# Block sums of x made early and kept in DRAM, and two column pairs moved into the block products

## The chip, the cores and the metric

One Trainium2 chip, of which the kernel uses one core. That core has a matrix engine (PE, with its weight loads shown apart as PEld), a vector engine (DVE), a scalar engine (ACT), GpSimd (POOL) and a queue engine (SP); SP, ACT and POOL issue DMA transfers. Each engine runs its instructions in the order of the program and waits on semaphores for what others make. The metric is the time of one execution on the device in microseconds, taken as the median of several runs. "The profile" is a page made from one execution that was recorded by the hardware; "the trace" is the record behind it.

## The reference, cut to what matters

All numbers are float32; the sequence has 1024 positions, the model 1024 channels.

```python
h = rms_norm(x, g_mix)
z = h @ w_in + b_in                       # 1024 -> 1024+1024+1536+1536+1024+1024
va, ga, xb, gb, sa, sb = split(z)

u = va * sigmoid(ga)
u = causal_depthwise_conv(u, conv_a_w, conv_a_b)       # 31 taps
u = silu(layer_norm(u, ln_g, ln_b))                    # mean over 1024 channels
y_a = u @ w_a_out

v = causal_depthwise_conv(xb, conv_b_w, conv_b_b)      # 4 taps
v = rg_lru(v, ...)                                     # gates per head, a linear scan in position
y_b = (v * gelu(gb)) @ w_b_out

m = sigmoid(sa) * y_a + sigmoid(sb) * y_b
x = x + m @ w_o
x = x + square(relu(rms_norm(x, g_mlp) @ w_1)) @ w_2   # hidden width 4096
out = rms_norm(x, g_final)
```

In the recurrence `rg_lru`, a = exp(log_a) and the input is multiplied by sqrt(-expm1(2 log_a)); the kernel makes these with exponential, tanh and square root on ACT, and the scan itself on DVE.

## The kernel before, in words

Tiles have 128 partitions; channels lie on partitions and positions along the free dimension. A product in full precision is made of three passes: each operand is split into a high part in the format fp32r and a low part (the rest), and high by high, high by low and low by high are added up. The high part is a copy on ACT. The low part is either a subtraction on DVE, or (`split_dma`, L64) a negated copy on ACT to which POOL's accumulating DMA adds the source.

Matrix `w_in` is used in column chunks of 128 columns, named by what they yield: VA and GA (8 chunks each), XB and GB (12 each), SA and SB (8 each).

*First part* (up to 360 us of the span). The list `CH` has 28 chunks: all of XB, VA and GA. A slot `s` of the loop multiplies one chunk (`chunk_mm`, 48 matmuls of 128x512), loads the weights of the chunk two slots on (`w_load`, SP), and splits those of the next (`w_parts`). In the same slots the gates of the 16 heads are multiplied (`head_mm`, at the slots `HS0`), the four-tap convolution is made (`xb_out`, `xb_parts`), and the scans follow group by group, three tiles to a group: `scan_exp` (exponential and tanh), `scan_root` (square root), `scan_in` and `scan_tile` (DVE; the result goes to DRAM tensor `hd`). `EXP` and `lag` say in which slots. A VA chunk and its GA chunk give, by `u_out`, the tile `ut[j]`, the input of the 31-tap convolution.

The convolution `conv(j)` is two steps on ACT and then 48 small ones on DVE, most of 128x512; its result `y` is stored in DRAM tensor `yd`, and POOL adds `yd[j]` into one tile `ysum` (`sum_up`, L603 to L609). The steps are fillers: the kernel writes the order of all engines by hand (`manual_schedule`) with a planner that keeps an estimated time for each engine (`clk`), a list of DVE steps with a time at which they are ready (`later`), and `vector_work`, which issues what is ready up to a given time and fills the rest with convolution steps, unless `taps["hold"]` is set. The planner's times set the order only.

*Second part* (360 to about 630 us). The chunks of GB, SA and SB are multiplied in pairs (`ZPAIRS`, 14 pairs of neighbours) by a block scheme with seven products in place of eight. The order is `zseq`, and each entry is one product of 12 matmuls (`z_mm`). The right operands are blocks of x, or sums of blocks, in high and low parts (`xbh`, `xbl`): products 1, 2 and 3 use the blocks themselves (`xh`, `xl`), products 7, 6, 5 and 4 use sums. The left operands are blocks of the weights or sums of them (`z_load`, `z_sums`, `z_lhs`; tiles `zw`, `zs`, `zo`). `z_post` copies one bank of PSUM into the next (bank "a" to "b" after product 1, "b" to "e" after product 6, where products 5 and 3 are added), and `z_out` applies gelu (GB; multiplied into the scan's result and stored in `hgd`) or sigmoid (SA, SB; stored in `gates`). A bank that is opened by a copy gets a filler matmul first in the first two pairs (`z_bank`).

The sums of blocks of x are made as follows. Normalised x (`xc`, eight tiles) is stored in DRAM tensor `xu` in slot 3. In slots 23 and 25 `x_load` brings back four tiles each, `x_sum` makes four subtractions on DVE a slot later, and `x_parts` splits the sums in slots 25 to 27 and at steps 0, 2 and 4 of `zseq`. Group 3 of the scans has its exponentials in slot 23, its roots a slot later, and its last tile at step 7 of `zseq`.

*Third part.* The output product of the recurrent branch, `b_mm(j)`, j = 0 to 7, of 72 matmuls each. In the middle of j = 2 two pairs of matmuls over `ysum` give the mean of the convolution (`n_parts`, `n_mean`, L1149); then the convolution's tiles `q`, loaded from `yd`, are centred (`n_center`), and at the start of j = 4 `n_var` makes the variance (L1149 again). Then come the product with `w_a_out`, `w_o` and the MLP, which the change does not touch.

Of the kernel before, what the change touches and what calls it, by code (L numbers as in the profile page):

```python
# [15 lines left out]
P = 128  # L16
# [15 lines left out]
def trunk_kernel(ctx: ExitStack, tc: tile.TileContext, x, xt_in, xt_eo, vecs, w_in, w_a_out, w_b_out,  # L32
# [87 lines left out]
    ep = stage.enter_context(tc.tile_pool(name="extra", bufs=1))  # L120
# [285 lines left out]
    xu = dp.tile([2, 4, P, S], F32, name="xu")  # L406
# [75 lines left out]
    def xb_parts(t):  # L482
        if t % 3 == 2:
            vp_[t] = tuple(qp.tile([P, S], F32R, tag="p", name=f"vt{x}{t}", bufs=4) for x in "hl")
        else:
            vp_[t] = T(f"vth{t}", F32R), T(f"vtl{t}", F32R)
# [64 lines left out]
    def scan_exp(g):  # L551
        at("A", 1.28)
        for t in range(3 * g, 3 * g + 3):
# [113 lines left out]
    xq = {}  # L667

    def x_load(c2):

        xq[c2] = {n: ep.tile([P, S], F32, tag="e", name=f"xs{n}_{c2}") if (n, c2) == (21, 0) else T(f"xs{n}_{c2}")
                  for n in (11, 12, 22, 21)}
        for n, a in xq[c2].items():
            nc.sync.dma_start(a, xu[n % 10 - 1, 2 * (n // 10 - 1) + c2])

    def x_sum(c2, ready):
        q = xq[c2]
        for n, a, b in ((11, 12, 11), (12, 22, 12), (22, 22, 11), (21, 21, 22)):
            later(ready, 1.2, nc.vector.tensor_tensor, q[n], q[a], q[b], ALU.subtract)

    def x_parts(c2, *ps):
        for p in ps:
            src = xq[c2][{6: 22, 7: 12, 5: 11, 4: 21}[p]]
            xbh[p][c2] = h = T(f"xs{p}h_{c2}", F32R)
            xbl[p][c2] = l = T(f"xs{p}l_{c2}", F32R)
            if c2 == 0 and p < 6:
                split_dma(src, h, l)
                at("A", 2.0)
            else:
                nc.scalar.activation(h, src, AF.Copy)  # L690
                later(at("A", 1.0), 1.2, nc.vector.tensor_tensor, l, src, h.bitcast(F32),
                      ALU.subtract)

    CH = [XB, VA, GA, XB + 1, XB + 2]
    for js, g in (((1,), 1), ((2,), 2), ((3,), 3), ((4, 5, 6, 7), 4)):
        CH += [c for j in js for c in (VA + j, GA + j)]
        CH += [XB + t for t in range(3 * g, min(3 * g + 3, 12))]
# [41 lines left out]
    ZPAIRS = [GB + 2 * i for i in range(6)] + [SA + 2 * i for i in range(4)]  # L739
    ZPAIRS += [SB + 2 * i for i in range(4)]  # L740
# [4 lines left out]
    def z_load(i, kk):  # L745

        zraw[i, kk] = raw = qp.tile([P, 2, 4, P], F32, tag="p", name=f"zw{i}_{kk}", bufs=4)
        c = ZPAIRS[i]
# [1357 lines left out]
```

## Time and profile before

| | |
|---|---|
| median of 3 runs | 1548.86 us (1547.82 to 1549.61) |
| the profiled execution | 1549.04 us, of which the recorded span is 1547.2 us |
| PE busy | 1535.6 us, 6804 instructions |
| DVE busy | 1214.5 us |
| ACT busy | 903.6 us |
| POOL busy | 188.6 us |
| start of the block products | 360.57 us |
| end of the first output block of the recurrent branch | 645.1 us |
| the mean's first matmul | 668.7 us |

The page gives the busy time of each engine over the whole span; the stages differ, so a table of busy times by stage is read beside it. A row of the view in order of time has start, duration, engine, line, operation, output and input, and in brackets how long the engine was idle before it and what ended that. Several instructions of one kind in a row are put together, with their count. A line of the waits names the waiting engine and instruction, what it waited for, the sum, the count and the longest.

### The profile page before, as it was taken

The numbers are of one execution on the slowest core, as the hardware profiler recorded it, in microseconds if no ns is written. First come the engines' busy times: TensorE is split into PE (matmuls) and PEld (weight loads), VectorE is DVE, ScalarE is ACT, GpSimd is POOL, SyncE is SP. The second block draws the span as 40 slices with busy tenths as digits, with TensorE's granted clock in tenths as the row PEclk, the third lists the DMA queues.
The fourth block names the chain that finished last, engine by engine and source line by source line (L and its number), as shares of the span: only waits on it lengthen the run. The fifth ranks groups of instructions, "written<-read, shape, count | busy, mean of one in ns | idle before, by whom it ended". The sixth has DMA issues, their size and how long they took to land. (4 is left out here: it accounts for less than half of the span.)

```text
span 1547.2 us, 19086 instructions
## 1 busy us (share of the span) xinstructions
PE 1535.6 (99%) x6804; PEld 1264.6 (82%) x6804; DVE 1214.5 (78%) x1641; ACT 903.6 (58%) x1266; POOL 188.6 (12%) x226
## 2 busy tenths in 40 slices
PE   9999999999999999999999999999999999999998
PEld 7878888788888888888888887888888888888886
DVE  6999989999899983468568868765555558888897
ACT  6748677576667667435375777545444475555553
POOL 0000000002222222000022322000000001111110
PEclk9999999999999999999999999999999999999999
DMA  8653554678999889854579978523333779888852
GB/s 348 169 127 95 160 140 134 158 227 214 264 267 256 195 206 259 270 196 126 185 195 306 194 171 198 211 75 124 113 115 111 242 216 229 226 223 223 205 124 109
DMA packets 124943, 294.18 MB, mean 190 GB/s; under 512 B 12464, under 2 KB 30512, under 8 KB 124848
## 3 DMA queue, kind: packets, MB, share of 16 engines
q1 hardware_dynamic: 93312, 213.00, 40.7%
q0 software_dynamic: 31392, 79.71, 28.1%
q8 instruction: 53, 0.87, 0.2%
q14 instruction: 42, 0.34, 0.1%
q10 hardware_dynamic: 144, 0.26, 0.1%
HBM read 152.93 MB, written 58.72 MB: 137 GB/s over the span
## 5 line engine op out<-in xcount | busy, mean ns | idle before, releaser
L735 PE MATMUL z<-xh,win_h 128*128 128x512 f32 x400 | 125.0, 390 | 0.0
L735 PE MATMUL z<-xl,win_h 128*128 128x512 f32 x400 | 123.5, 390 | 0.0
L1873 DVE TENSOR_TENSOR acc<-acc,d 128x1024 f32<-128x1024 f32 x72 | 87.8, 1220 | 33.4 <-PE d L1861 32.7
L735 PE MATMUL z<-xh,win_l 128*128 128x512 f32 x400 | 99.4, 391 | 0.0
L735 PEld LDWEIGHTS z<-xh,win_l 128*128 128x128 f32 x400 | 75.2, 188 | 16.8
L735 PEld LDWEIGHTS z<-xh,win_h 128*128 128x128 f32 x400 | 75.1, 188 | 16.5 <-ACT win_h L68 0.4
L648 DVE SCALAR_TENSOR_TENSOR y<-u,vec,y 128x511 f32<-128x511 f32 (+14 forms) x120 | 88.5, 737 | 0.0
L735 PEld LDWEIGHTS z<-xl,win_h 128*128 128x128 f32 x400 | 75.1, 188 | 15.8
L648 DVE SCALAR_TENSOR_TENSOR yt<-u,vec,yt 128x511 f32<-128x511 f32 (+6 forms) x112 | 82.6, 737 | 0.0
L648 DVE SCALAR_TENSOR_TENSOR y<-yt,csum,y 128x511 f32<-128x511 f32 (+6 forms) x112 | 82.6, 737 | 0.0
L542 ACT ACTIVATE g<-rg,vec 96x1024 f32<-96x1024 f32 x32 | 35.6, 1113 | 79.6 <-PE rg L532 79.6
L1540 ACT ACTIVATE o<-s 128x512 fp32r<-128x512 f32 x58 | 34.7, 623 | 52.8 <-DVE s L1525 31.3
L67 POOL DMA_DIRECT2D win_l<-win_raw x25 | 21.6, 865 | 319.1 <-ACT win_l L66 248.4
L476 DVE SCALAR_TENSOR_TENSOR v<-xb,vec,v 128x1023 f32<-128x1023 f32 (+2 forms) x36 | 46.2, 1282 | 11.4 <-ACT v L467 10.4
L67 POOL DMA_DIRECT2D zo<-zw x42 | 36.2, 862 | 133.6 <-ACT zo L66 125.3
L1121 PE MATMUL yb<-hgl,wb_h 128*128 128x512 f32 x168 | 51.8, 390 | 0.0
L1121 PE MATMUL yb<-hgh,wb_h 128*128 128x512 f32 x168 | 51.8, 389 | 0.0
L66 ACT ACTIVATE zo<-zw 128x512 fp32r<-128x512 f32 x42 | 26.3, 626 | 30.7 <-DMA zw<-in_w_in_dram 8.7
L67 POOL DMA_DIRECT2D db_1l<-wr x7 | 6.0, 860 | 309.8 <-DMA wr<-in_w_dram 254.0
L1121 PE MATMUL yb<-hgh,wb_l 128*128 128x512 f32 x168 | 41.0, 390 | 0.0
L1085 DVE TENSOR_TENSOR o<-s,o 128x512 fp32r<-128x512 f32 x58 | 38.8, 682 | 0.0
L1121 PEld LDWEIGHTS yb<-hgh,wb_h 128*128 128x128 f32 x168 | 31.6, 188 | 6.5
(1795 smaller groups left out, 4672.9 us busy)
## 6 DMA issues: line engine op xcount, KB each, us to landing
w_raw<-in_w_dram SPq DMA_DIRECT2D x36, 512.0 KB, 5.5
fr<-fd SPq DMA_DIRECT2D x32, 512.0 KB, 5.9
wr<-in_w_dram SPq DMA_DIRECT2D x32, 512.0 KB, 6.5
zw<-in_w_in_dram SPq DMA_DIRECT2D x28, 512.0 KB, 5.9
win_raw<-in_w_in_dram SPq DMA_DIRECT2D x25, 512.0 KB, 4.1
win_l<-win_raw POOLq DMA_DIRECT2D x25, 512.0 KB, 4.5
zo<-zw POOLq DMA_DIRECT2D x42, 256.0 KB, 5.6
gates<-zg SPq DMA_DIRECT2D x32, 256.0 KB, 4.0
```

The costliest lines, as they stand in the source:

```text
L66: nc.scalar.activation(l, src, AF.Copy, scale=-1.0)
L67: nc.gpsimd.dma_start(l, src, accum_op=ALU.add)
L476: nc.vector.scalar_tensor_tensor(v[:, d:S], a[:, 0:S - d], cbw_c[:, w * 12 + t:w * 12 + t + 1], v[:, d:S], ALU.mult, ALU.add)
L542: nc.scalar.activation(a, gps.pop((n, gi))[:HD, :], AF.Sigmoid, bias=(ba_c, bx_c)[gi][:, n:n + 1])
L648: nc.vector.scalar_tensor_tensor(o[:, k:], a[:, 0:HS - k], c, o[:, k:], ALU.mult, add)
L735: nc.tensor.matmul(zps[s][:, HALVES[hf]], w[:, k, :], xw[k][part][hf], start=n == 0, stop=n == 23)
L1085: tt(l, src, h.bitcast(F32), ALU.subtract)
L1121: nc.tensor.matmul(ps[hf], a, b[:, HALVES[hf]], start=n == 0, stop=n == len(todo) - 1)
L1540: nc.scalar.activation(o[:, 0], src, AF.Copy)
L1873: tt(acc[p, q2], acc[p, q2], ps, ALU.add)
```

## The change

The sums of blocks of x are made in slots 4 and 6, in place, on the tiles `xc` themselves (`x_sum`), and `xu`, `x_load` and `x_parts` go. `x_make`, in slots 5 to 7, writes the sums to a new DRAM tensor `xsd`: those for products 7 and 6 as a high part (copied by ACT, stored by a DMA that ACT issues) and a low part (subtracted by DVE, stored by SP); those for products 5 and 4 as they are. The stores on SP are collected and issued once a slot (`x_store`). `x_get` loads the parts for product 6 in the last slot and those for product 7 ahead of the block products. `x_raw` loads the sums for products 5 and 4 at steps 0 and 5 of `zseq`, and `x_split` splits them at steps 3 and 4, and 7 and 8 (ACT for the high part, DVE for the low one).

`CH` has 24 chunks: VA and GA number 6 and 7 leave it. They become pairs 6 and 7 of 16 in `ZPAIRS`, each with its VA chunk as the first and its GA chunk as the second of the pair; `z_load` reads them with a stride. `z_branch` forms the convolution's input from the results, and `z_joined` hands it to the planner when both halves are there.

The exponentials of scan tiles 9 and 10 stand in the last slot but one, that of tile 11 at step 2 of `zseq`, the three roots at step 4, and the scans of the tiles at steps 5, 11 and 15. Convolution steps are held back in the first twelve steps of `zseq` rather than two. One filler matmul is left. Four tiles of `xb_parts` come from another pool. The first left operands are made before the last matmuls of the last slot.

```diff
     wp = stage.enter_context(tc.tile_pool(name="weights", bufs=2))
-    ep = stage.enter_context(tc.tile_pool(name="extra", bufs=1))
...
-    xu = dp.tile([2, 4, P, S], F32, name="xu")
+    xsd = dp.tile([4, 2, 2, P, S], F32, name="xsd")
...
     def xb_parts(t):
-        if t % 3 == 2:
+        if t in (2, 5, 8, 9):
...
-    def scan_exp(g):
-        at("A", 1.28)
-        for t in range(3 * g, 3 * g + 3):
+    def scan_exp(g, part=range(3)):
+        if 0 in part:
+            at("A", 1.28)
+        for t in (3 * g + n for n in part):
...
-    xq = {}
-
-    def x_load(c2):
-
-        xq[c2] = {n: ep.tile([P, S], F32, tag="e", name=f"xs{n}_{c2}") if (n, c2) == (21, 0) else T(f"xs{n}_{c2}")
-                  for n in (11, 12, 22, 21)}
-        for n, a in xq[c2].items():
-            nc.sync.dma_start(a, xu[n % 10 - 1, 2 * (n // 10 - 1) + c2])
-
-    def x_sum(c2, ready):
-        q = xq[c2]
-        for n, a, b in ((11, 12, 11), (12, 22, 12), (22, 22, 11), (21, 21, 22)):
-            later(ready, 1.2, nc.vector.tensor_tensor, q[n], q[a], q[b], ALU.subtract)
-
-    def x_parts(c2, *ps):
-        for p in ps:
-            src = xq[c2][{6: 22, 7: 12, 5: 11, 4: 21}[p]]
-            xbh[p][c2] = h = T(f"xs{p}h_{c2}", F32R)
-            xbl[p][c2] = l = T(f"xs{p}l_{c2}", F32R)
-            if c2 == 0 and p < 6:
-                split_dma(src, h, l)
-                at("A", 2.0)
-            else:
-                nc.scalar.activation(h, src, AF.Copy)
-                later(at("A", 1.0), 1.2, nc.vector.tensor_tensor, l, src, h.bitcast(F32),
-                      ALU.subtract)
-
-    CH = [XB, VA, GA, XB + 1, XB + 2]
-    for js, g in (((1,), 1), ((2,), 2), ((3,), 3), ((4, 5, 6, 7), 4)):
-        CH += [c for j in js for c in (VA + j, GA + j)]
-        CH += [XB + t for t in range(3 * g, min(3 * g + 3, 12))]
+    def x_sum(c2):
+        q11, q12, q22, q21 = (xc[i + c2] for i in (0, 4, 6, 2))
+        for o, a, b in ((q11, q12, q11), (q12, q22, q12), (q22, q22, q11), (q21, q21, q22)):
+            later(clk["P"] - 7, 1.2, nc.vector.tensor_tensor, o, a, b, ALU.subtract)
+
+    def x_make(c2, p):
+        src = xc[{5: 0, 7: 4, 6: 6, 4: 2}[p] + c2]
+        if p in RAW:
+            stored.append((xsd[p - 4, c2, 0], src))
+            return
+        h, l = (T(f"xs{p}{n}_{c2}", F32R) for n in "hl")
+        nc.scalar.activation(h, src, AF.Copy)
+        nc.scalar.dma_start(xsd[p - 4, c2, 0], h.bitcast(F32))
+        later(at("A", 1.1), 1.2, nc.vector.tensor_tensor, l, src, h.bitcast(F32), ALU.subtract)
+        stored.append((xsd[p - 4, c2, 1], l.bitcast(F32)))
+
+    stored = []
+
+    def x_store():
+        for a in stored:
+            nc.sync.dma_start(*a)
+        stored.clear()
+
+    def x_get(c2, p):
+        for n, a in enumerate((xbh, xbl)):
+            a[p][c2] = T(f"xb{p}{'hl'[n]}_{c2}", F32R)
+            nc.sync.dma_start(a[p][c2].bitcast(F32), xsd[p - 4, c2, n])
+
+    def x_raw(c2, p):
+        xbl[p][c2] = T(f"xb{p}l_{c2}", F32R)
+        nc.sync.dma_start(xbl[p][c2].bitcast(F32), xsd[p - 4, c2, 0])
+
+    def x_split(c2, p):
+        xbh[p][c2], l = T(f"xb{p}h_{c2}", F32R), xbl[p][c2]
+        nc.scalar.activation(xbh[p][c2], l.bitcast(F32), AF.Copy)
+        later(at("A", 1.06), 1.2, nc.vector.tensor_tensor, l, l.bitcast(F32), xbh[p][c2].bitcast(F32),
+              ALU.subtract)
+
+    NJ = 6
+    CH = [XB + 0, VA + 0, GA + 0, XB + 1, XB + 2, VA + 1, GA + 1, XB + 3, XB + 4, XB + 5, VA + 2, GA + 2, XB + 6, XB + 7, XB + 8, VA + 3, GA + 3, XB + 9, XB + 10, XB + 11, VA + 4, GA + 4, VA + 5, GA + 5]
...
-    ZPAIRS = [GB + 2 * i for i in range(6)] + [SA + 2 * i for i in range(4)]
-    ZPAIRS += [SB + 2 * i for i in range(4)]
+    ZPAIRS = [(c, c + 1) for c in range(GB, SB + 8, 2)]
+    ZPAIRS[6:6] = [(VA + j, GA + j) for j in range(NJ, 8)]
...
         zraw[i, kk] = raw = qp.tile([P, 2, 4, P], F32, tag="p", name=f"zw{i}_{kk}", bufs=4)
-        c = ZPAIRS[i]
-        nc.sync.dma_start(raw, w_in[c:c + 2, :, 4 * kk:4 * kk + 4, :].rearrange("m p k c -> p m k c"))
+        c, d = ZPAIRS[i]
+        nc.sync.dma_start(raw, w_in[c:d + 1:d - c, :, 4 * kk:4 * kk + 4, :].rearrange("m p k c -> p m k c"))
...
                mybir.EngineType.SP, mybir.EngineType.Pool}
-    HS0 = [4 + 5 * (n // 4) + n % 4 for n in range(NH)]
+    HS0 = [(4, 9, 14, 19)[n // 4] + n % 4 for n in range(NH)]
     head_at = {s: n for n, s in enumerate(HS0)}
-    EXP = {head_slot: g for g, head_slot in enumerate(HS0[4 * g + 3] + 1 for g in range(4))}
-    XL = {23: 0, 25: 1}
-    XS = {25: ((x_parts, 0, 6),), 26: ((x_parts, 0, 7, 5),), 27: ((x_parts, 0, 4),)}
+    EXP = {head_slot: g for g, head_slot in enumerate(HS0[4 * g + 3] + 1 for g in range(3))}
+    RAW = (4, 5)
+    XS = {4: ((x_sum, 0),), 5: ((x_make, 0, 5), (x_make, 0, 7)), 6: ((x_make, 0, 6), (x_make, 0, 4), (x_sum, 1)),
+          7: tuple((x_make, 1, p) for p in (5, 7, 6, 4)),
+          NC1 - 2: ((scan_exp, 3, (0, 1)),),
+          NC1 - 1: ((scan_in, 0, 9, 10), (x_get, 0, 6), (x_get, 1, 6))}
     w_load(3)
     head_w(0)
     w_load(4)
-    for c2 in range(4):
-        nc.sync.dma_start(xu[1, c2], xc[4 + c2])
     w_parts(3)
     with tc.manual_schedule(engines=ENGINES):
         for s in range(3, NC1):
             w_load(s + 2)
-            if s in XL:
-                x_load(XL[s])
...
                 head_mm(before, 1)
+            if s == NC1 - 1:
+                z_get(0, z_lhs)
+                z_get(1, z_lhs)
             if s > 3:
                 chunk_mm(s, 18, 24)
+            x_store()
...
                     g = EXP[s - d]
-                    lag = int(g < 3)
+                    lag = 1
...
                     t = 3 * g + d - 2 - lag
-                    if 3 * g <= t < 3 * g + 3 and t < 11:
+                    if 3 * g <= t < 3 * g + 3 and t < 10:
                         later(rooted[t], 4.8, scan_tile, t)
-            if s == NC1 - 1:
-                z_get(0, z_lhs)
-                z_get(1, z_lhs)
-            if s - 1 in XL:
-                x_sum(XL[s - 1], max((r for r, *_ in todo), default=0))
+            if s == NC1 - 2:
+                for i in range(4):
+                    z_load(i // 2, i % 2)
             for f, *a in XS.get(s, ()):
                 f(*a)
-            if s == NC1 - 3:
-                for i in range(4):
-                    z_load(i // 2, i % 2)
-            if s == 3:
-                for c2 in range(4):
-                    nc.sync.dma_start(xu[0, c2], xc[c2])
...
         zb[i, b] = t = zp.tile([P, HS], F32, tag="z", name=f"z{i}{b}")
-        if i < 2 and b in "be":
+        if i == 0 and b == "b":
...
     def z_out(i, m_, hf, src, name):
-        ci = ZPAIRS[i] + m_
+        ci = ZPAIRS[i][m_]
         bias = bin_c[:, ci:ci + 1]
-        if ci < SA:
+        if ci < XB:
+            z_branch(ci, hf, src, bias)
+        elif ci < SA:
...
+    zu, zg = {}, {}
+
+    def z_branch(ci, hf, src, bias):
+        j = ci % GA
+        if j not in zu:
+            zu[j] = T(f"u{j}")
+        d, g = halved(zu[j], hf), src.rearrange("p (n o) -> p o n", o=2)
+        if ci >= GA:
+            zg[j, hf] = g
+            nc.scalar.activation(src, src, AF.Sigmoid, bias=bias)
+            ready = at("A", 0.62)
+            if hf == 0:
+                later(ready, 0.63, nc.vector.tensor_tensor, d, d, g, ALU.mult)
+                z_joined(j)
+        elif hf == 0:
+            nc.scalar.activation(d, g, AF.Identity, bias=bias)
+            at("A", 0.62)
+        else:
+            later(0, 0.68, nc.vector.scalar_tensor_tensor, d, g, bias, zg.pop((j, hf)), ALU.add, ALU.mult)
+            z_joined(j)
+
+    def z_joined(j):
+        if j in ut:
+            fresh.append(j)
+        ut[j] = zu[j]
+
     hb = {}
     def z_h(i, m_, hf):
-        t = ZPAIRS[i] + m_ - GB
-        if t < 12:
+        t = ZPAIRS[i][m_] - GB
+        if 0 <= t < 12:
...
-    ZX = {0: ((x_parts, 1, 7),), 7: ((later, 0, 4.8, scan_tile, 11),), 2: ((x_parts, 1, 5),), 4: ((x_parts, 1, 4),)}
+    ZX = {0: ((x_raw, 0, 5), (x_raw, 1, 5)), 2: ((scan_exp, 3, (2,)),), 3: ((x_split, 0, 5),), 4: ((x_split, 1, 5), (scan_root, 3),),
+          5: ((later, 0, 4.8, scan_tile, 9), (x_raw, 0, 4), (x_raw, 1, 4)), 7: ((x_split, 0, 4),), 8: ((x_split, 1, 4),), 11: ((later, 0, 4.8, scan_tile, 10),),
+          15: ((later, 0, 4.8, scan_tile, 11),)}
...
         z_get(3, z_lhs)
-        u_out(7, zps[NC1 - 2], zps[NC1 - 1])
-        x_parts(1, 6)
+        u_out(NJ - 1, zps[NC1 - 2], zps[NC1 - 1])
+        scan_in(0, 11)
         vector_work(clk["V"])
+        for c2 in range(2):
+            x_get(c2, 7)
...
                     f(*a)
-            taps["hold"] = n < 2
+            taps["hold"] = n < 12
```

## The prediction

> **What bounds the kernel now.** I read the page first, then the waits of PE, a table of the span by stage, and then, at two places, the order in time.
>
> ```profile
> span 1547.2 us, 19086 instructions
> PE 1535.6 (99%) x6804; PEld 1264.6 (82%) x6804; DVE 1214.5 (78%) x1641; ACT 903.6 (58%) x1266; POOL 188.6 (12%) x226
> ```
> ```profile
> PE spare L345 <- POOL ones L114: 1.6, 1, 1.6
> PE gu4a L1297 <- ACT u_late L1351: 1.6, 1, 1.6
> ```
> ```profile
> 43.00:97.00 54.00, 54.00 (x238) 43.72 (x237) 51.88 (x90) 32.32 (x39) 3.67 (x5) 1.00 0.58 151
> 360.00:580.00 220.00, 219.84 (x971) 181.79 (x970) 202.53 (x310) 143.31 (x245) 55.11 (x64) 1.00 0.92 230
> 580.00:645.00 65.00, 65.00 (x287) 53.50 (x286) 28.67 (x32) 41.84 (x63) 10.36 (x12) 1.00 0.94 266
> ```
>
> PE is busy 99% of the span, and the two rows shown are its longest waits, 1.6 us each; neither lies where the change does. So two things can move the time: matmuls that go or come, and a new wait of PE. In the table by stage the columns after the window are PE, PEld, DVE, ACT, POOL, clock, DMA share and GB/s: the clock granted is full, 238 matmuls in 54.00 us make 0.2269 us for one, 971 in 220 make 0.2266. I take 0.2267. The same table gives the slack elsewhere: DVE is full up to 580 us (202.5 of 220) and idle for 36 of the 65 us after it. That gap is what the change uses up.
>
> **What goes and comes on PE.** Four column chunks of the first part go (VA and GA, 6 and 7), at 48 matmuls each: 192. Two pairs of block products come, each 7 products of 12 matmuls, twice over for two row halves, so 84 a pair: 168. Three of the four filler matmuls at the start of a bank go. Net 27 matmuls less at 0.2267 us: **-6.1 us**, all on the path, since PE never rests. The weight loads lie beside PE both times (PEld 82%).
>
> **The block sums.** The eight subtractions on whole x tiles, eight high parts on ACT and the low parts are as many as before, and only stand earlier. Eight stores and eight loads of 512 KB become twelve stores and twelve loads; four of the stores are issued by ACT.
>
> ```profile
> L656 SPq DMA_DIRECT2D yd<-y x8: 319/341/434, 108.0 to 576.2; - x8
> ```
> ```profile
> xu<-xc SPq DMA_DIRECT2D x8, 512.0 KB, 6.5
> xs<-xu SPq DMA_DIRECT2D x8, 512.0 KB, 8.1
> ```
> An issue on SP took 0.32 to 0.43 us, so ACT pays about 1.4 us over three slots, while it is busy 32.3 of 54 us in the stretch 43 to 97: nothing. The two low parts that were built by an accumulating DMA (POOL) now cost two more DVE steps, of the kind of ysuml below (1.22 us). In slots 4 to 8 DVE is nearly full (51.88 of 54), but most of it is filler, steps of the convolution placed where there is room: what comes in pushes those later. The twelve stores stand on SP ahead of weight loads that are issued two slots (a chunk's 48 matmuls alone are 10.9 us a slot) ahead of use; a store of this size landed in 6.5 us, so they are covered, at zero, unless SP stands a whole slot waiting for a low part (a rival below). The loads of the stored parts are issued a slot or more ahead of their use and landed in 8.1 us in the old form: zero.
>
> **Where block products begin.** Counted from the first block product, Z = 360.57 in the old trace:
>
> ```profile
> 360.57 0.39 PE L933 MATMUL z0a<-xh,zo 128*128 128x512 f32 x1
> 380.29 0.39 PE L933 MATMUL z0e<-xs5h,zo 128*128 128x512 f32 x1
> 386.41 0.39 PE L933 MATMUL z0e<-xh,zo 128*128 128x512 f32 x1
> ```
> ```profile
> 366.66 0.58 ACT L971 ACTIVATE z1b<-z1a 128x512 f32<-128x512 f32 x1
> 367.45 0.64 ACT L776 ACTIVATE zo<-zs 128x512 fp32r<-128x512 f32 x1 [0.21 <-DVE zs L453]
> 367.99 1.04 ACT L690 ACTIVATE xs5h<-xs 128x1024 fp32r<-128x1024 f32 x1
> 369.05 1.28 ACT L945 ACT_TABLE_LOAD   x1
> 370.34 0.69 ACT L945 ACTIVATE ze<-z0a,vec 128x512 f32<-128x512 f32 x1
> ...
> 375.05 0.58 ACT L974 ACTIVATE z0e<-z0b 128x512 f32<-128x512 f32 x1
> ```
> ```profile
> 329.03 2.96 ACT L564 ACTIVATE g<-g 128x1024 f32<-128x1024 f32 x3
> ```
> ```profile
> L557 ACT ACTIVATE g<-g,sm 128x1024 f32<-128x1024 f32 x12 | 13.9, 1155 | 0.4
> L556 ACT ACTIVATE a<-g,c 128x1024 f32<-128x1024 f32 x12 | 13.7, 1142 | 0.0
> ```
> The product into bank z0e, due at Z+19.7, needs ACT's copy z0b to z0e, which stood at Z+14.5. In the new order ACT does, from z1b (Z+6.1) on: z1b 0.5, a weight part 0.5, a table load 1.28, exponential and tanh of scan tile 11 (1.15 each), a table load 1.28, a gelu 0.6, a weight part 0.55, the high part of x for block 5 (1.0), a gelu 0.6, two weight parts 1.06, the other high part 1.0, a table load 1.28, three square roots 2.96. That is 14.9 us, so the copy starts at Z+21.0 and ends at Z+21.6: PE waits **1.9 us**. Behind the copy stand, on ACT, zu0 and the parts of the weight sum for the third product of the bank; in the old trace POOL issued that sum's accumulating transfer 1.9 us after the copy's start:
>
> ```profile
> 376.94 0.86 POOL L67 DMA_DIRECT2D zo<-zs  x1 [2.18 <-ACT zo L66]
> ```
> ```profile
> zo<-zw POOLq DMA_DIRECT2D x42, 256.0 KB, 5.6
> zo<-zs POOLq DMA_DIRECT2D x28, 256.0 KB, 6.9
> ```
> So it is issued at Z+22.9 and lands 5.6 to 6.9 us later, at 28.5 to 29.8, where PE wants it at Z+25.8 (386.41). The two waits are one chain, and the later end counts: 2.7 to 4.0 us; if the transfer keeps ahead, the 1.9 alone; if ACT overlaps better than I sum, less. I take **+3.3** (range 1 to 4).
>
> [...]
>
> **The convolution's end and the mean.** Tiles 6 and 7 of the convolution's input now come out of the block products, the seventh and eighth pairs of sixteen, and taps are held back for the first twelve products rather than two. In the new order the last 20 DVE steps of tile 7 stand behind the last hidden parts, fifteen of them between the second low part of weight block 1 and the first sum sb. Before, they were done at 576.2, 92 us ahead of the mean:
>
> ```profile
> 575.50 0.69 DVE L655 TENSOR_TENSOR y<-y,yt 128x511 f32<-128x511 f32 x1
> ```
> ```profile
> 559.72 0.73 DVE L648 SCALAR_TENSOR_TENSOR y<-yt,csum,y 128x501 f32<-128x501 f32 x1
> 560.37 0.73 DVE L648 SCALAR_TENSOR_TENSOR yt<-u,vec,yt 128x501 f32<-128x501 f32 x1
> ```
> ```profile
> 639.18 1.83 DVE L1085 TENSOR_TENSOR wb_l<-wb_raw,wb_h 128x768 fp32r<-128x768 f32 x2 [0.16 <-ACT wb_h L1099]
> 645.12 1.29 DVE L1128 TENSOR_TENSOR sb<-yb,sb 128x512 f32<-128x512 f32 x2 [4.11 <-PE yb L1121]
> ```
> ```profile
> 668.96 0.40 PE L1150 MATMUL mu<-ysuml,onesr 128*128 128x512 f32 x1
> ```
> ```profile
> L609 POOL DMA_DIRECT2D ysum<-yd x1: 1220/1220/1220, 594.8 to 594.8; - x1
> L1159 ACT ACTIVATE ysumh<-ysum x1: 1044/1044/1044, 649.3 to 649.3; 128x1024 fp32r<-128x1024 f32 x1
> L1085 DVE TENSOR_TENSOR ysuml<-ysum,ysumh x1: 1224/1224/1224, 650.4 to 650.4; 128x1024 fp32r<-128x1024 f32 x1
> ...
> DMA to landing us min/median/max: 6.1/6.1/6.1
> ```
> Count from E = 645.1, the end of the first output block. The low parts end at E-4.1; fifteen taps at 0.65 end at E+5.7; sb 1.3, the next pair of low parts 1.8, two taps and three tile sums 3.3 (0.65 to 0.7 each): tile 7 is finished at E+12.2. Then it is stored to DRAM, added by POOL's accumulating DMA into ysum, split by ACT (1.04) and DVE (1.22), and PE wants the low part at 668.96, E+23.8. All landings of these two transfers, tile y and then tile ysum:
>
> ```profile
> DMA to landing us min/median/max: 2.6/4.0/8.7
> ```
> ```profile
> DMA to landing us min/median/max: 6.1/8.7/9.6
> ```
> With the medians: 12.2 + 4.0 + 8.7 + 2.3 = E+27.2, **+3.4 us** of PE waiting. With the shortest (2.6, 6.1) E+23.2: nothing. With the longest (8.7, 9.6) E+32.8: 9.0. I take the medians: in the old trace the last accumulation took 6.1 with nothing beside it of its own chain, in the new order sixteen loads of the convolution's blocks stand on SP just behind the store, and run beside it. What is queued behind: on ACT the high parts of weight block 3, on DVE the sums of the second output block and block 3's low parts, due at about E+33: they end at about E+30, covered. The chain to the variance starts from the mean and moves with it.
>
> **The rest.** The last scans move among the first sixteen products and push taps, already counted by the order. The other banks go without filler: no engine waits for that.
>
> **Sum**: -6.1 + 3.3 + 3.4 = +0.6 on the profiled execution's 1549.04; that stands 0.18 above the median of the runs, 1548.86, so about **1549.5**. Faster or slower than 0.2% (3.1 us) is about what a measurement of this kernel can tell from no change.
>
> **Rivals.**
> 1. *The waits are hidden* (faster). If landings are as short as the shortest rows and ACT's chain ends in time for bank z0e, the 6.1 us stay, less the part of z's start that can't be hidden (0 to 2.5): 1543 to 1545.5. For it: the last ysum row took 6.1, and the shortest landings leave E+23.2 against 23.8. Against: the ACT chain is a sum of measured steps.
> 2. *The mean waits longer* (slower). The place is the store of tile 7 and its accumulation, beside sixteen 256 KB loads. It decides when the two landings together exceed 15.3 us (12.2 + 15.3 + 2.3 - 23.8 = 6.0, and -6.1 + 3.3 + 6.0 passes 3.1); with 8.7 for each, 17.4, the mean waits 8.1 and the sum is +5.3: about 1554. Against: the medians make 12.7. [...]
> 3. *The early slots break* (slower). SP stands in slots 5 to 8 at a store of a low part that DVE has not made, and a weight load behind it comes late; x's tiles are held longer by the stores. One late weight block costs up to a landing, 6.5: 1556. For it: DVE 96% busy there. Against: two slots of cover.
> [...]
>
> **Chances.** Forecast (both waits partly there, net within 0.2%) 0.36; rival 1 0.34; rival 2 0.18; rival 3 0.09; rival 4 0.03. So faster 0.34, same 0.36, slower 0.30. The forecast's own range is 1546 to 1552; the range over the cases goes from the better half of rival 1 to the middle of rivals 2 and 3: 1543.5 to 1555.5.
>
> **What would show it.** In the new profile: 27 matmuls of 128x512 fewer; in PE's waits a line of z0e on ACT's copy of about 2 us and one on the transfer of zo of 1 to 2; a line of mu on ACT's ysumh or DVE's ysuml of about 3.4; DVE full up to the first output block. The forecast is wrong if the waits of PE are the old ones (then 1543), if one of the two is twice its size, or if PE waits in slots 4 to 10 of the first part.

## The result

The changed kernel takes 1565.81 us (median of four runs, 1564.31 to 1567.27) against 1548.45 us before: a ratio of 1.0111, with a 95% interval of 1.0097 to 1.0124. It is slower by 17 us, outside the range, and on the side to which the prediction gave 0.30. The profiled execution took 1566.92 us, with a span of 1565.1 us against 1547.2. Each time below is the median of a version's fast runs; r14 has only one (1549.67 us), as its other run took 2207 us at a granted clock of 0.65.

From the page of the changed kernel, the line of busy times and the clock line of the forty slices (before, the clock line holds only nines):

```profile
PE 1537.8 (98%) x6777; PEld 1262.7 (81%) x6777; DVE 1227.6 (78%) x1661; ACT 911.8 (58%) x1291; POOL 192.6 (12%) x230
PEclk9999999989999999999999999999999999999999
```

PE has the 27 instructions less that the sum counted on, and is busy 2 us longer. The longest waits of PE in the changed kernel (total in us, times, longest):

```profile
PE z0e L937 <- ACT z0e L1006: 6.8, 1, 6.8
PE mu L1185 <- ACT ysumh L1195: 3.6, 1, 3.6
PE spare L344 <- POOL ones L114: 1.6, 1, 1.6
PE z15e L937 <- ACT zc L1014: 1.5, 1, 1.5
PE z0a L937 <- DMA zo<-zw: 1.3, 1, 1.3
...
PE z0f L937 <- DMA xb7l<-xsd: 1.0, 2, 0.8
...
PE mu L1186 <- DVE ysuml L1121: 0.8, 1, 0.8
PE yb L1157 <- DVE hgl L452: 0.5, 1, 0.5
PE yb L1157 <- ACT hgh L1057: 0.5, 1, 0.5
```

Both places of the prediction are there. The start of the products waits more than twice as long as was priced. Rows of the view of one tile give the marks in time from which I count: the first product (z0a) and the ninth pair (z8a), of before and then of after, and for after the mean and the variance (the last two numbers in front of the semicolon are the first and last start):

```profile
L933 PE MATMUL z0a<-xh,zo x16: 388/389/390, 360.6 to 369.0; 128*128 128x512 f32 x16
L933 PE MATMUL z8a<-xh,zo x16: 388/390/390, 508.8 to 522.2; 128*128 128x512 f32 x16
```
```profile
L937 PE MATMUL z0a<-xh,zo x16: 389/389/500, 316.5 to 326.3; 128*128 128x512 f32 x16
L937 PE MATMUL z8a<-xh,zo x16: 389/389/389, 477.4 to 490.8; 128*128 128x512 f32 x16
L1185 PE MATMUL mu<-ysumh,onesr x2: 495/562/628, 682.2 to 684.0; 128*128 128x512 f32 x2
L1185 PE MATMUL var<-vah,onesr x2: 393/394/394, 712.5 to 712.9; 128*128 128x512 f32 x2
```

| stretch | before | after | difference | of it work |
|---|---|---|---|---|
| up to the first product | 360.6 | 316.5 | -44.1 | -43.5 (four chunks) |
| first product to ninth pair | 148.2 | 160.9 | +12.7 | -0.7 (three fillers) |
| ninth pair to the mean | 159.9 | 204.8 | +44.9 | +38.1 (two pairs) |
| mean to variance (695.0 before) | 26.3 | 30.3 | +4.0 | 0 |
| variance to the end of the span | 852.2 | 852.6 | +0.4 | 0 |

So 13.4 us are lost at the start of the products and 10.8 around the mean, for 6.1 us of matmuls saved. More is lost than the waits add up to. The stages of the changed kernel (the columns as in the prediction; the clock is the third from the right):

```profile
330.00:340.00 10.00, 8.29 (x34) 5.76 (x32) 2.88 (x5) 3.63 (x7) 0.00 (x0) 1.00 0.94 369
340.00:345.00 5.00, 0.00 (x0) 0.00 (x0) 3.07 (x4) 4.97 (x6) 0.86 (x1) 0.64 0.76 163
345.00:350.00 5.00, 3.89 (x9) 3.15 (x10) 4.82 (x5) 5.00 (x9) 1.72 (x2) 0.50 0.67 206
684.00:690.00 6.00, 6.00 (x16) 4.67 (x15) 5.90 (x9) 2.28 (x4) 0.00 (x0) 0.54 0.89 297
```

After each of the two long waits PE runs for some 5 us at about half the granted clock (0.50 and 0.54 above): the 12 matmuls of the product behind the first wait took from 346.11 to 351.39, 5.28 us in place of 2.72.

**What is late at the start.** ACT in order of time, and below it SP's issue of the load in question:

```profile
330.71 0.62 ACT L785 ACTIVATE zo<-zs 128x512 fp32r<-128x512 f32 x1
337.69 1.06 ACT L701 ACTIVATE xb5h<-xb5l 128x1024 fp32r<-128x1024 f32 x1 [6.36 <-DMA xb5l<-xsd]
...
341.33 1.28 ACT L564 ACT_TABLE_LOAD   x1
342.62 2.95 ACT L564 ACTIVATE g<-g 128x1024 f32<-128x1024 f32 x3
345.48 0.58 ACT L1006 ACTIVATE z0e<-z0b 128x512 f32<-128x512 f32 x1
```
```profile
328.73 1.57 SPq L697 DMA_DIRECT2D xb5l<-xsd  x2
```

ACT stands 6.4 us for block 5 of x (the sum for product 5), whose load SP issued only 12 us after the first product. The roots that the prediction named come behind that. What kept SP is seen in the transfers between 300 and 340 us (KB each, median us to landing):

```profile
xb6l<-xsd SPq DMA_DIRECT2D x2, 512.0 KB, 18.1
xb7l<-xsd SPq DMA_DIRECT2D x2, 512.0 KB, 15.5
hd<-g SPq DMA_DIRECT2D x2, 512.0 KB, 14.1
xb5l<-xsd SPq DMA_DIRECT2D x2, 512.0 KB, 8.9
```

The stores and loads of the sums, 512 KB each, landed in 6.5 and 8.1 us before; the loads for products 6 and 7 now take 15 to 18 (medians). From 16.5 us ahead of the first product to 23.5 behind it 12.2 MB were moved, at a DMA share of 0.93, and at shares of 0.94 to 1.08 from 310 us on; in the same stretch of before, 344 to 384 us, it was 9.0 MB at 0.88. In SP's order the two transfers of block 5 stand eight places behind the last load for product 6 and eight behind a store of `hd`, and in the trace SP waited for just these two before it issued them (2.3 and 0.9 us). So slow landings hold back the issue of what comes later.

### The profile page after: what moved, and what is told of

It reads as the page before. It is cut to its first block, busy times and chain, and to the rows that moved or that the text cites. A ratio compares the mean times of both kernels' runs of the same rounds, so it can differ in the third digit from the quotient of the medians.

```text
span 1565.1 us, 19115 instructions
## 1 busy us (share of the span) xinstructions
PE 1537.8 (98%) x6777; PEld 1262.7 (81%) x6777; DVE 1227.6 (78%) x1661; ACT 911.8 (58%) x1291; POOL 192.6 (12%) x230
## 4 chain that ended last, share of the span: by engine, by line
PE 88%; DMA 6%; DVE 2%; ACT 2%; issue 1%; SPq 0%; POOL 0%; DVEq 0%; POOLq 0%; ACTq 0%
PE d L1897 15%; PE z L744 14%; PE yb L1157 6%; PE e L2014 3%; PE keep L1897 2%; PE z L257 2%; DMA hg<-hgd 1%; DMA xb6l<-xsd 1%; PE rg L529 1%; PE rg L531 1%; PE rg L530 1%; DMA hb<-hd 1%; DMA w_raw<-in_w_dram 1%; DMA ysum<-yd 1%; DMA zo<-zs 1%
## 5 line engine op out<-in xcount | busy, mean ns | idle before, releaser
L744 PE MATMUL z<-xh,win_h 128*128 128x512 f32 x336 | 105.0, 390 | 0.0
L744 PE MATMUL z<-xl,win_h 128*128 128x512 f32 x336 | 103.7, 389 | 0.0
L744 PE MATMUL z<-xh,win_l 128*128 128x512 f32 x336 | 84.2, 391 | 0.0
L744 PEld LDWEIGHTS z<-xh,win_l 128*128 128x128 f32 x336 | 63.1, 188 | 14.4
L744 PEld LDWEIGHTS z<-xh,win_h 128*128 128x128 f32 x336 | 63.1, 188 | 13.7
L744 PEld LDWEIGHTS z<-xl,win_h 128*128 128x128 f32 x336 | 63.1, 188 | 13.3
L67 POOL DMA_DIRECT2D zo<-zw x48 | 41.6, 867 | 166.6 <-ACT zo L66 154.3
L67 POOL DMA_DIRECT2D win_l<-win_raw x21 | 18.2, 868 | 275.1 <-ACT win_l L66 214.5
L66 ACT ACTIVATE zo<-zw 128x512 fp32r<-128x512 f32 x48 | 30.0, 626 | 25.9 <-issue 6.2
L67 POOL DMA_DIRECT2D zo<-zs x32 | 27.7, 865 | 92.6 <-ACT zo L66 90.0
```

The costliest lines, as they stand in the source:

```text
L67: nc.gpsimd.dma_start(l, src, accum_op=ALU.add)
L744: nc.tensor.matmul(zps[s][:, HALVES[hf]], w[:, k, :], xw[k][part][hf], start=n == 0, stop=n == 23)
```

## The experiments

Two pairs of theories. At the start: (A) the loads pile up, against (B) group 3's steps on ACT do it alone. At the mean: (C) the convolution is late because its steps are held back for twelve products, against (D) DVE has no room for them. The stretch below is always from the first product to the ninth pair: 148.2 before, 160.9 in the changed kernel. It is read from the one profiled execution of each version, and that one took up to 2.8 us more than the median (r7), so differences of 1 or 2 us between stretches carry nothing. Two more versions were written, r2 (group 3's steps on ACT and DVE all at steps 11 to 20) and r4 (r1, r2 and r3 together); in both the engines would wait for each other in a circle, so they gave no time, and r9 takes up the question of r2.

**r1: loads a slot or two earlier.**

```diff
-          NC1 - 1: ((scan_in, 0, 9, 10), (x_get, 0, 6), (x_get, 1, 6))}
+          NC1 - 3: ((x_get, 0, 6), (x_get, 1, 6)), ...
+          NC1 - 1: ((scan_in, 0, 9, 10), (x_get, 0, 7), (x_get, 1, 7))}
-            x_get(c2, 7)                                      # ahead of the products
+            x_raw(c2, 5)                                      # no longer at step 0
```


> Only the place of the loads changes: the parts for product 6 are loaded two slots earlier, those for product 7 in the last slot, and the raw sums for product 5 ahead of the block products. Theory A (the loads pile up: all transfers between 305 and 340 us share engines that are full): 2 MB leave the pile, about 6 us at 0.35 MB/us, so the loads of block 5 land that much earlier, ACT's wait for them (6.4 us) goes to 0 to 1, PE's wait at z0e from 6.8 to about 1 to 2.6, and the time falls by 5 to 9 us to 1557 to 1561. Theory B (the scan's steps on ACT are the cause, the loads beside them): PE's wait at z0e stays above 5 us and the time within 2 us of 1565.8.

Measured: 1561.6 us (before 1547.7 beside it), just above A's range; stretch 157.7. As A has it, ACT no longer waits for block 5 and the wait at z0e falls to 2.1. But the first pair's weights are now behind these loads on SP:

```profile
PE z0a L937 <- DMA zo<-zw: 4.1, 1, 4.1
PE mu L1185 <- ACT ysumh L1195: 2.5, 1, 2.5
PE z0e L937 <- ACT z0e L1006: 2.1, 1, 2.1
```

**r3: the hold of convolution steps two products long, as before.**

```diff
-            taps["hold"] = n < 12
+            taps["hold"] = n < 2
```


> Only the hold of convolution steps is shortened from twelve to two steps of the products, as in the kernel before. Theory C (tile 7 of the convolution is late because DVE idled beside the first products, 8 of 25 us used between 320 and 345): its 20 last steps are done before the first output block, the waits at the mean (3.6 and 0.8 us, and some 2.5 us at half the clock behind them) go, and the time falls by about 6 us to 1560. Theory D (DVE has no room: the steps delay the sums and products of the first block pairs): the wait at the mean goes but new waits of PE on DVE come among the first products, and the time stays within 2 us of 1565.8.

Measured: 1554.87 us, 10.9 less than the changed kernel, where 6 were expected. In this order of the steps C holds and D falls: all that was lost behind the ninth pair is back (mean at 674.2, 197.6 us from the ninth pair; 159.9 + 38.1 is 198.0), and the waits at z15e and yb are gone too, which I had not put down to it. But the hold is not the cause by itself, as r9 and r18 show further down. What goes with the late mean is the place of tile 7's last step: in the four versions with a late mean (the changed kernel, r1, r18, r19) DVE does it behind the first sum `sb` and the next low parts, in all others ahead of them. The changed kernel had 20 steps left behind the second low part of weight block 1, of which 15 stand ahead of `sb` and 5 behind; r3 had 11, all ahead. The stretch at the start stays at 160.1. The longest waits left:

```profile
PE z0e L937 <- ACT z0e L1006: 6.8, 1, 6.8
PE z0a L937 <- DMA zo<-zw: 1.6, 1, 1.6
```

**r5, r6, r7: r3 with the roots one step later; also the first pair's weights a slot earlier; also the loads of r1.**

```diff
-          4: ((x_split, 1, 5), (scan_root, 3),), 5: ((later, ..., scan_tile, 9), ...
+          4: ((x_split, 1, 5),), 5: ((scan_root, 3), (later, ..., scan_tile, 9), ...    # r5
-            if s == NC1 - 2:                        # z_load of pairs 0 and 1
+            if s in (NC1 - 3, NC1 - 2):             # pair 0, pair 1          r6
```


> The short hold of r3_hold, and the three roots of group 3 one step later, so that ACT makes the copy into bank z0e before them. Theory A (loads): ACT still waits 4 to 5 us for the load of block 5, but the table load and the roots (1.28 + 2.96) no longer stand between the second high part and the copy, so PE's wait at z0e falls from 6.8 to 2 to 3 us, the half clock behind it gets shorter, and the time falls by 4 to 6 us from 1554.9 to about 1550. Theory B (the scan's steps alone): the wait at z0e falls to below 0.5.

> r5_root, and the two loads of the first pair's weights issued a slot earlier, ahead of SP's wait (11 us) for the gates of head 14. Theory A: 1 MB leaves the pile between 305 and 335 us, the other loads land about 3 us earlier, PE's wait at z0a (1.3 to 1.6) goes, that at z0e falls by 2 to 3 us; 2 to 4 us less than r5_root. Theory B: no change beyond 1 us.

> r6_zw, and the loads of product 6 two slots earlier, those of product 7 in the last slot, those of block 5 ahead of the products (the edit of r1_load). Theory A: 3 MB in all have left the pile; block 5 is there before ACT wants it, no wait of PE above 1 us remains at the start of the products, and the time is 1548.5 - 6.1 plus 1 to 3 us: 1543 to 1546, below the kernel before. If the pile is not the cause, 1549 or more.

Measured: 1557.64, 1553.44 and 1554.64 us; stretches 162.5, 159.3 and 161.6. The wait at the copy into z0e falls to 2.6 and then vanishes, as A has it. But the roots now stand between the copy and the next step of ACT, and the third product of the bank waits. The rows of r6:

```profile
PE z0e L937 <- ACT zc L1014: 4.2, 1, 4.2
...
PE z0a L937 <- DMA zo<-zw: 1.4, 1, 1.4
```

r5 was expected 4 to 6 us below r3 and came out 2.8 above it; r6 is 4.2 below r5, about as forecast; r7 was expected at 1543 to 1546 and missed by 9 us.

**r8: the block sums without the moved pairs.** `NJ = 8` and the four chunks back at the end of `CH`.

> The first part of the change without the second: VA and GA 6 and 7 stay in the first part (28 chunks, 14 pairs), the early block sums, the later scans and the long hold as in the changed kernel. The 24 matmuls saved by the two pairs are gone. Theory A: the loads pile up all the same, and the start of the products loses about 10 us as in the changed kernel. Theory C: tile 7's input is there before the products, but with the long hold the mean is still late by some microseconds, or not at all if DVE catches up in 14 pairs. So 1558 to 1566; if it comes near 1548, the moved pairs are what made the loads and the mean late.

Measured: 1551.71 us against 1548.11, a ratio of 1.0023 (1.0011 to 1.0034); stretch 151.4. The guess of 1558 to 1566 was wrong, and this run shows what makes the loads late: here there are four slots more between the last heads and the products, and SP issues the loads early.

```profile
344.40 0.45 SPq L693 DMA_DIRECT2D xb6h<-xsd  x1
...
349.08 0.39 SPq L693 DMA_DIRECT2D xb7l<-xsd  x1
361.55 0.85 SPq L697 DMA_DIRECT2D xb5l<-xsd  x2
```
```profile
PE z0e L937 <- ACT z0e L1006: 2.1, 1, 2.1
```

Product 6's first load stands 16 us ahead of the first product (360.4) and product 7's last one 11; in the changed kernel they go from 9.9 us ahead to 4.3 behind, since SP stands at the gates of head 14 up to 303.2 us first (the row of their transfers is 11.35 us long). Block 5 is issued 1.2 us behind the first product, not 12. ACT waits for no load, its copy into z0e starts 20.9 us behind the first product (21.0 was forecast), and what is left is the 2.1 us that its own chain costs. So of the 13.4 us lost at the start 3.9 belong to the first part of the change by the same count (151.4 against 148.2, with three fillers less): this wait and the half clock behind it (0.62 from 381.9 to 385.0 us). The other 9.5 come only when the pairs are moved as well. The moved pairs without the early sums were not run. The mean is in time here, 159.6 us from the ninth pair, although the hold is twelve products.

**r9 to r12: group 3's steps on ACT moved.** r9 is the changed kernel with roots of tiles 9 and 10 at step 1, exponential and root of tile 11 at steps 11 and 13, and scans at steps 2, 5 and 16; r10 adds the hold of r3 and the weights of r6; r11 makes the first product's weight parts ahead of the exponentials; r12 adds the loads of r1.

> The changed kernel with only group 3's steps on ACT moved: the roots of tiles 9 and 10 at step 1 of the products, exponential and root of tile 11 at steps 11 and 13 (scans of the tiles at steps 2, 5 and 16). Between the start of the products and the copy into z0e ACT then has 9 us less to do. Theory A (loads): block 5 lands no earlier (about 337 us), ACT waits for it longer, and PE still waits 2 to 3 us at z0e; about 1561, with the late mean unchanged. Theory B (scan steps): the wait at z0e is below 0.5, about 1556.

> Short hold, the first pair's weight loads a slot earlier, and group 3's steps on ACT moved as in r9. If loads and ACT together make the start of the products late, both PE waits at z0e (copy 6.8, third product 4.2 in r6_zw) fall below 1, 1.4 us stay at z0a: 1548.1 - 6.1 plus 2 to 4 us with a little half clock: 1544 to 1546.5. If new waits take their place, 1549 or more.

> r10, and the first product's weight parts made ahead of the exponentials of tiles 9 and 10 on ACT. The wait at z0a (1.4 us for the low part's transfer) goes: 1 to 2 us below r10.

> r11, and the loads of product 6 two slots earlier, of 7 one slot and of block 5 ahead of the products, as in r1_load. In r1_load and r7_all these loads held SP and with it the gates and the second pair's weights by 3 us, and PE waited 3.4 to 4.1 us at z0a. If that wait was due to the first product's weight parts, it is gone now and the time is that of r11 or 1 us less; if it was due to the later gates, it stays, and the time is 2 to 4 us above r11.

Measured: 1559.25, 1556.94, 1557.78 and 1555.56 us; stretches 164.2, 160.5, 164.3 and 162.0. In r9 ACT has an exponential, a tanh, a root and table loads less ahead of the copy, and only waits the longer for block 5; PE still waits 2.5 us, and B alone falls. That the time comes near A's 1561 is luck, though: the stretch grew to 164.2, and what came back is the mean, 197.7 us from the ninth pair, which A expected to stay late. The hold is twelve products long as in the changed kernel, but only 13 steps of tile 7 were left, and all stand ahead of `sb`. The row of ACT:

```profile
337.80 1.06 ACT L701 ACTIVATE xb5h<-xb5l 128x1024 fp32r<-128x1024 f32 x1 [8.04 <-DMA xb5l<-xsd]
```

In r10 the wait at the copy is gone, and others have come, on sums of DVE and on the weights of later pairs:

```profile
PE z1f L937 <- DVE zc L452: 2.8, 1, 2.8
...
PE z0a L937 <- DMA zo<-zw: 1.4, 1, 1.4
PE z2a L937 <- DMA zo<-zw: 1.3, 1, 1.3
```

Of r10's two branches (1544 to 1546.5, or 1549 and more with new waits) the second came. r11 was expected 1 to 2 us below r10 and came out 0.8 above; r12 came out 2.2 below r11, in neither of its branches. From r3 to r12, but for r8, the stretch stayed at 159 to 164.

**r13, r14: bytes taken away.** r3 without the loads for product 7 (it uses the parts of product 6), and without those and the splits for products 5 and 4 too.

```diff
-            x_get(c2, 7)
+            xbh[7][c2], xbl[7][c2] = xbh[6][c2], xbl[6][c2]
```


> r3_hold without the four loads (2 MB) of the parts for product 7: it uses those of product 6 in their place, so part of the output is not the reference's. Theory A, in its stronger form (the first 60 us of the products are bound by the bytes that the DMA engines must move, and re-ordering only moves the waits): from the first product to the ninth pair's first product r3_hold takes 160.1 us where the kernel before takes 148.2; without 2 MB, about 6 us at 0.33 MB/us, it takes 153 to 156, and the time falls to 1548 to 1551. Theory B (ACT's and DVE's work decides, loads are beside it): no change beyond 2 us.

> As r13, and also without the loads and splits for products 5 and 4 (another 2 MB, four copies on ACT, four subtractions on DVE); they use the parts of product 6, so the output is not the reference's. Theory A: that stretch takes about 148 to 150 us, no wait of PE above 2 us is left but what ACT's scan steps make, and the time is 1543 to 1545. Theory B: the wait at z0e stays at 2 to 4 us for the scan's steps.

Measured: 1550.74 us (in the range) and 1549.67 us (a single run, 5 us above its range); stretches 156.1 and 153.7. Two MB are worth 4.0 us, the next two with their splits 2.4. The longest waits of r13, then of r14:

```profile
PE z0e L937 <- ACT z0e L1006: 3.4, 1, 3.4
```
```profile
PE z0a L941 <- DMA zo<-zw: 1.6, 1, 1.6
...
PE z0e L941 <- ACT z0e L1010: 1.5, 1, 1.5
```

The strong form of A, under which 4 MB less would give 148 to 150, falls: 5.5 us stay. Of the 11.9 us that r3 loses in the stretch, 4.0 go with two MB of loads, and most of the rest can be read from r13's trace. There ACT waits for no load ahead of z0e; its chain is that of the prediction with two convolution steps (1.4 us) that the short hold lets in, and PE waits 3.4 us for it. The two products behind that wait take 8.3 us in place of 5.4, so the half clock costs 2.9, and the wait at z0a is 1.5: together 7.8 of the 7.9 us left (8.6 with the fillers). In r14 the two high parts of block 5 are gone from the chain as well, and the wait is 1.9 us shorter. Whether r13's 4.0 us are the bytes themselves stays open: the loads of block 5 landed no faster (14.1 us, median, against 8.9 in the changed kernel), but SP issued them at 318.1 us instead of 327.2 in r3, with four loads less ahead of them.

**r15, r16: all four sums stored raw (`RAW = (4, 5, 6, 7)`), 2 MB fewer loads; r16 with the weights of r6 and the scan steps of r9.**

> r3_hold with all four sums stored raw (RAW 4 to 7): loads of 4 MB rather than 6, those of 6 three slots from the end and those of 7 in the last; all splits at the products' start. 2 MB less and 2 MB earlier: theory A says the loads no longer bind and the rest is ACT's scan chain (two high parts and four roots' worth more work than the room there): z0e waits 3 to 5 us for ACT, 1548 to 1551.

> r15 with the first pair's weights loaded a slot earlier and group 3's steps on ACT moved as in r9. Theory A: 1543 to 1547, below the kernel before (1548.1). If waits on the weight transfers of later pairs come in their place as in r12, 1550 or more.

Measured: 1553.63 us (above its range) and 1557.74 us (the second branch); stretches 155.9 and 161.4. In the stretch r15 gains what r13 gained, with the work kept; but its first product starts at 318.2 us instead of r3's 316.5, so the time is only 1.2 us below r3's. PE waits 3.6 us at z0e for ACT, which has four more high parts and two more convolution steps there than in the changed kernel. r16 gives the gain back (waits of 2.6 us at z3a and 1.8 at z2a, both for weights).

**r17 to r19: scans of tiles 9 and 10 back at steps 5 and 11, tile 11's steps on ACT together at step 13**, on r10, on r16, and on r16 with the weights late again.

> r10 with the scans of tiles 9 and 10 back at steps 5 and 11 and tile 11's exponential and root together at step 13. In r10 DVE had the two scans (4.8 us each) among the first products and SP stood at their stores; if these made its waits at z1f (2.8, on a sum of DVE) and z2a (1.3, on later weights), they go, and the stretch from the first product to the ninth pair takes 154 to 157 us instead of 160.5: 1550 to 1553. If the bytes alone bind, it stays at 159 to 161.

> r17 with all four sums stored raw, as in r15 (2 MB fewer loads). Bytes and scan steps are both out of the first products: the stretch takes 149 to 152 us, and the time is 1543.5 to 1547, below the kernel before. If it stays above 154, some other order (weights of the first pairs behind the gates on SP) binds.

> r18 with the first pair's weight loads back in the last slot but one, behind SP's wait for the gates: 1 MB more in the pile. By the theory of bytes 1 to 3 us above r18, with PE's wait at z0a back at 1.5.

Measured: 1554.61, 1563.95 and 1565.14 us; stretches 160.1, 159.4 and 158.8. In r17 the third pair starts 37.2 us behind the first product (45.9 in the changed kernel, 33.5 before), and then the rest is lost between the third and the fifth pair, which take 46.1 us instead of 38.1, with

```profile
PE z3b L937 <- DMA zo<-zs: 2.7, 1, 2.7
PE z1f L937 <- DVE zc L452: 1.8, 1, 1.8
```

r18 and r19 bring the late mean back as well (680.7, 203.5 and 204.0 us from the ninth pair), though their hold is two products long: r18 had 17 of tile 7's steps left, 15 ahead of `sb` and 2 behind. r17's stretch took the second branch, r18 missed its range by 17 us, and r19 came out 1.2 us above r18, as forecast.

One pattern runs through these versions. Where group 3's steps are moved as in r9 or r17 (r9 to r12, r16 to r19), it takes 36.0 to 40.7 us from the first product to the third pair, and 44.6 to 48.8 from there to the fifth. With these steps as in the changed kernel or one step from there (the changed kernel, r1, r3, r5, r6, r7, r13, r15) it takes 40.8 to 45.9 and 38.2 to 40.9; before, 33.5 and 38.1. So what is saved in the first stretch is lost again in the second. Whether the moved steps themselves do that, or the weights and sums of the third and fourth pairs come no earlier whatever stands ahead of them, no run tells.

No version here that computes all beats the kernel before. The nearest is r8, and of those with the moved pairs r6 and r15, which can't be told apart (1553.44 and 1553.63).

## Why the prediction was wrong

*Matmuls saved, -6.1 us*: right. 27 instructions fewer; the first product comes 44.1 us earlier for 43.5 of chunks.

*The block sums, "the loads of the stored parts are issued a slot or more ahead of their use and landed in 8.1 us in the old form: zero"*: this step failed. "A slot or more" (10.9 us) does not hold for the last loads even in the program: block 5 is loaded at step 0 and split at steps 3 and 4, three to four products (8.2 to 10.9 us) later. By the prediction's own sum ACT comes to it 13.1 us behind the first product, so that the load had to be issued 5 us behind it at the latest. And the old landing time was taken for loads that now start together with the first weights, the scans' stores and head 14's gates. Those for products 6 and 7 landed in 14 to 20 us; SP issued block 5 only 12.2 us after the first product, and ACT stood 6.4 us for it, so that PE's wait at z0e was 6.8 us. The step looked at each load and not at what stands around it: the loads of before stood in a stretch with a DMA share of 0.69 (300 to 340 us), and the four loads of the first weights right behind them were already slow in the old trace:

```profile
zw<-in_w_in_dram SPq DMA_DIRECT2D x4, 512.0 KB, 19.2
```

Bytes alone would not have told: around the first product the share was 0.88 before and 0.93 after, for 226 and 305 GB/s. Nor did the step ask what the four slots that leave had hidden; r8 shows that with them the loads are in time and the wait is 2.1 us, r1 that it is 2.1 us too when they are issued earlier. None of the rivals had this. What no version found is an order with the moved pairs that loses neither to the loads nor to ACT's chain nor further on.

*ACT's chain to z0e, 1.9 us*: the mechanism was right, and so was its size where the loads don't cover it: 2.1 us in r8, and 3.4 in r13 with 1.4 us of convolution steps in the chain. In the changed kernel the 6.4 us for block 5 come on top, and the copy ends 29.5 us behind the first product, where 21.6 was forecast; PE itself was late by then, with 2.3 us of waits at z0a and z0f. The second half of that term, the transfer of the third product's weights, did not show.

*The table loads at 1.28 us each*: right. The three of that chain, at 325.18, 328.83 and 341.33, took 1.28 us each, and ACT's next instruction started 1.29 or 1.30 us after the start of each (1.29 in the old rows, 369.05 to 370.34).

*The mean, +3.4 us*: the place and the chain were right to about 1 us. Counted from the first output block's end (654.9 in the new trace) tile 7 is finished at 11.9 (12.2 forecast), its store landed in 3.5 us (4.0), its accumulation in 9.8 (8.7).

```profile
666.15 0.68 DVE L655 TENSOR_TENSOR y<-y,yt 128x511 f32<-128x511 f32 x1
```
```profile
682.19 0.49 PE L1185 MATMUL mu<-ysumh,onesr 128*128 128x512 f32 x1 [3.58 <-ACT ysumh L1195]
683.45 0.80 PE L1186 MATMUL mu<-ysuml,onesr 128*128 128x512 f32 x1 [0.77 <-DVE ysuml L1121]
```

The wait is 4.4 us, 1.0 more than forecast. What the sum lacked is the rest of the 10.8: half the clock behind it (0.54 from 684 to 690 us; about 3 us up to the variance), and 2.5 us of waits ahead of it, at the last pair and the first output block. All of it goes in r3; that these 2.5 us come from the late DVE is not shown (ACT waits for the loads of `hg` there).

*Rival 2* had this place but wanted long landings for it; they took 13.3 us together where it set in at 15.3. *Rival 3*, the early slots, did not happen: nothing is lost before the first product.

*The bound of a wait*: the sum counted a wait of PE at its length. Both long waits cost 2.5 to 3 us more than that, by the clock (0.50 and 0.54). In all, 13.4 us were lost at the start where the sum had 3.3, and 10.8 around the mean where it had 3.4.

## What to carry to other kernels

When work leaves a stage, look at what that stage was hiding: list everything that must be issued and land in the first tens of microseconds of the next one, in the order of its queue, and take landing times from the place in the trace where the transfers are as dense, rather than from a quieter one. When every re-ordering only moves the wait, take work away (bytes, copies) in an experiment before trying another order, and read stage by stage where the wait went. And price a wait of the matrix engine with what follows it.

## What the runs showed of the hardware

PE's clock. After waits of 6.8 and 3.6 us the granted clock was 0.50 (345 to 350 us) and 0.54 (684 to 690 us), and a product took 5.28 us instead of 2.72. In r8 it also fell behind a wait of 2.1 us:

```profile
381.90:385.00 3.10, 3.06 (x9) 2.42 (x10) 3.07 (x3) 3.10 (x7) 1.62 (x2) 0.62 0.37 130
```

Behind 1.3 us at z0a and 1.5 us at z15e in the changed kernel the clock stayed at 1.00 (318 to 322 and 633 to 635 us). In other runs the rows of PE show it by the time from one matmul's start to the next, which is 0.22 to 0.24 us in these two places of the changed kernel and 0.42 or 0.43 in most of the product of 5.28 us. It rose to 0.42 or 0.43 behind waits of 3.1 us (r5), 3.4 (r13, r7), 4.1 (r1) and 4.2 (r6, r7). Behind waits of 1.0 to 1.6 us (r3, r5, r6, r9 to r12) it stayed at 0.22 to 0.24, but for the first step and a few gaps. Between these the rows show both: 0.43 from 1.3 us on behind waits of 2.10 us (z0e in r8) and 2.60 us (z0e in r5), and 0.22 to 0.24, again but for the first step, in the product behind waits of 1.87 us (z0e in r11) and 2.54 us (z0e in r9).

Landings under load. A load of 512 KB for product 6 or 7 took 14 to 20 us to land in the changed kernel, where the engines' share was 1.06 (310 to 330 us); in r8 the same loads took 5.2 to 7.6 for product 6 and 11.9 to 15.4 for the low parts of product 7. SP's loads and POOL's transfers of weights grew late together here (POOL's from medians of 5.6 and 6.9 us over the whole of before to 8.1 and 9.9 between 300 and 340 us).
